# Mixing products put behind the preceding dense step, one product for the cached forget sums, and a vector's load moved to POOL

## The chip, the cores and the metric

One core of one Trainium2 chip runs one inference step. The metric is the device time of one execution in microseconds (us). Engines are named as in the profile: PE (TensorE, products), ACT (ScalarE), DVE (VectorE), POOL (GpSimd), SP (SyncE, which only issues DMAs here).

## What is computed

A hybrid encoder of two layers steps 256 new frames of one stream and 16 frames of each of 8 running streams, which makes 384 tokens, three tiles of 128.

```python
# layer 0: one projection, two kinds of attention, one output projection
fq, fk, fv, fz, logf, sq, sk, sv, sz = ab_project(rmsnorm(h, norm0_g), w_in0, b_forget)
F_all = cumsum(concat([cache_fox_logf, logf]), axis=1)       # forget sums, cached rows included
go = fox_core(fq, k_all, v_all, F_all[:, P:], F_all, qpos, kpos)
to = sb_core(sq, sk_all, sv_all, qpos, kpos)
h  = h + concat([go * silu(fz), to * silu(sz)]) @ w_out0
# layer 1: gated MLP with mixing over positions
p  = rmsnorm(h, norm1_g) @ w_in1                              # u, v, z of 4096 columns each
u, v, z = p[..., :C], layernorm(p[..., C:2*C], ln_g, ln_b), p[..., 2*C:]
mixed = einsum('gts,bnsgc->bntgc', tril(w_sp), v) + b_sp      # 16 groups of 256 columns
h  = h + (u * mixed * silu(z)) @ w_out1
y  = rmsnorm(h, final_g)
```

Everything is fp32.

## The kernel before

All large products run as three products of parts: a value is split into `hi`, rounded by ACT (L84 for weights, L90 for activations), and `lo`, what DVE has left (L86 and L91). For each weight tile of 128x512 and each token tile, PE does hi by hi (L100), hi by lo of the weight (L101) and lo of the activation by hi (L102). `dense_nat` runs over pairs `kp` of weight tiles; a pair is 18 products. Weights come by SP into `raw` (five buffers), and `whi` and `wlo` have four buffers each, so ACT can split a weight tile only when PE is done with the fourth before it.

A scheduler sets the order on each engine from the program and its own estimate; `tc.issue_after(x)` orders an instruction behind `x` if both are on the same engine. Engines run strictly in that order.

The change touches the end of layer 1. The 4096 columns are worked in eight blocks of 512, by `prepare(c)`, a generator whose steps are hooked between the pairs of dense products by `first_plan` and `later_plan`:

- `load_v`, `normalise`: POOL loads v, DVE normalises it (L1159, L1160), POOL loads what it needs;
- `turned_weights`, `split_values`: w_sp is turned and split (`wTh`, `wTl`), v is split (`vh` by ACT, `vl` by DVE);
- mixing: twelve products on PE, L1258 (vh, wTh), L1259 (vl, wTh) and L1260 (vh, wTl), six with 512 columns and six with 256, in four banks `a`; DVE multiplies each bank into `gate` (L1262);
- POOL writes `gate` to memory as `md` (three DMAs, L1268) and reads it back as `blk` (four, L1271), in order to turn it;
- DVE turns blk into `gTt` (L1275), and ACT and DVE split that into two slots, the chunk's hi and lo (L90, L91), which are the weights side of the dense products with w_out1.

So block c of the mixing becomes chunk c of w_out1's products: `out1(0, 8)` takes chunks 0 and 1, `out1(8, 8)` 2 and 3, `out1(16, 8)` 4 and 5, `out1(24, 4)` 6. Ahead of `out1(16, 8)` POOL also loads the final norm's vector (two DMAs of final_g) and three tiles of the last weights (w_out1). `last_product` holds the last product of the last pair that the program has written.

The forget sums of the cached rows are in `forget()`: `clf` holds the cached logs as [128 positions, 8 streams, 8 heads]; eight fp32 products (L440), one for each head, multiply it with a triangle `UT`, and two evictions (L444) and two DMAs (L445) store the result. At the start, `graw` (norm0_g, 16x128) comes by ACT's queue (L232), is transposed by PE (L258) between the transpositions of x (L263) and copied to `gT`, which DVE uses when it evicts x; `keep_warm` (L226) adds products of ones that nothing reads.

Of the kernel before, what the change touches and what calls it, by code (L numbers as in the profile page):

```python
# [15 lines left out]
P = 128  # L16
# [21 lines left out]
def tile_hybrid_step(  # L38
# [96 lines left out]
                G.dma_start(dst[32 * j:32 * j + 32, :, 32 * a:32 * a + 32], trn[32 * a:32 * a + 32, :, 32 * j:32 * j + 32])  # L135


    ident = cpool.tile([P, P], F32, name="ident")
    make_identity(nc, ident)
    ones = cpool.tile([P, P], F32, name="ones")  # L140
# [28 lines left out]
    with ExitStack() as l0:  # L169
        lc = l0.enter_context(tc.tile_pool(name="l0c", bufs=1, reuse_waits="tile"))  # L170
        lp = l0.enter_context(tc.tile_pool(name="l0p", bufs=2, reuse_waits="tile"))

        graw = lc.tile([KT, 2, P], F32, name="graw")
        def gains(j):
            gb = bank()
            PE.transpose(gb[:, :KT], graw[:, j, :], ident[:KT, :KT])
# [51 lines left out]
        keep_warm(6)  # L228
        for half in range(2):
            load_piece(0, half, nc.scalar)  # L230
            if not half:
                nc.scalar.dma_start(graw[:, 0, :], norm0_g.rearrange("(k p) -> k p", p=P))  # L232
            load_raw()
        load_piece(1, None, nc.scalar)
        load_raw()
# [15 lines left out]
        def x_transposes(k):  # L251
            if k < FB:
                b = bank()
                for tb in range(NT):
                    if k == 0 and tb == 2:

                        gb = bank()
                        then("PE", lambda: PE.transpose(gb[:, :KT], graw[:, 0, :], ident[:KT, :KT]))  # L258
                        then("DVE", lambda: V.tensor_copy(gT[:, :KT], gb[:, :KT]))
                        keep_warm(1)  # L260
                        b2 = bank()
                    bt = b if k or tb < 2 else b2
                    then("PE", lambda: PE.transpose(bt[:, tb * P:(tb + 1) * P], xs[k // 4][:, tb, k % 4 * P:k % 4 * P + P], ident))  # L263
            else:
                b = xblk[k]
            gcol = gT[:, k:k + 1]
            hi, lo = hhi[k // 4][:, k % 4, :], hlo[k // 4][:, k % 4, :]
            if k:
                high = then("ACT", lambda: S.activation(hi, b[:, :T], AF.Copy, scale=gcol))
            else:  # L270

                parts = (b, slice(0, 2 * P)), (b2, slice(2 * P, T))
                for bt, ts in parts:
                    high = then("DVE", lambda: V.tensor_scalar(out=hi[:, ts], in0=bt[:, ts], scalar1=gcol, scalar2=None, op0=ALU.mult))
                for bt, ts in parts:
                    low = then("DVE", lambda: V.scalar_tensor_tensor(out=lo[:, ts], in0=bt[:, ts], scalar=gcol, in1=f32(hi[:, ts]), op0=ALU.mult, op1=ALU.subtract))
                return high, low
            return high, then("DVE", lambda: V.scalar_tensor_tensor(out=lo, in0=b[:, :T], scalar=gcol, in1=f32(hi), op0=ALU.mult, op1=ALU.subtract))
# [132 lines left out]
        def forget(o):  # L411
            z = lc.tile([P, NT, 8], F32, name="fz")
            for tb in range(NT):
                V.scalar_tensor_tensor(out=z[:, tb, :], in0=o[tb][:, 256:264], scalar=rstd[:, tb:tb + 1], in1=bfg, op0=ALU.mult, op1=ALU.add)
            e = lc.tile([P, NT, 8], F32, name="fe")
            S.activation(e, z, AF.Abs)
            S.activation(e, e, AF.Exp, scale=-1.0)
            S.activation(e, e, AF.Ln, bias=1.0)
            V.scalar_tensor_tensor(out=logf, in0=z, scalar=0.0, in1=e, op0=ALU.min, op1=ALU.subtract)
            G.dma_start(flf_p.rearrange("o (t p) h -> p (o t) h", p=P), logf[:, :2, :])  # L420
            G.dma_start(flf_s.rearrange("b q h -> (b q) h"), logf[:, 2, :])

            yield
            b3 = bank()
            PE.matmul(b3[:8, :2 * P], lhsT=logf[:, 0, :], rhs=UT, start=True, stop=False)
            PE.matmul(b3[:8, P:2 * P], lhsT=logf[:, 1, :], rhs=UT[:, :P], start=False, stop=True)
            bs = bank()
            PE.matmul(bs[:8, :P], lhsT=logf[:, 2, :], rhs=BT, start=True, stop=True)
            for b_ in range(8):
                PE.matmul(bs[:8, P + b_:P + b_ + 1], lhsT=clf[:, b_, :], rhs=ones[:, 0:1], start=True, stop=True)  # L430
            tot = lc.tile([8, 8], F32, name="ftot")
            V.tensor_copy(tot, bs[:8, P:P + 8])
            FT = lp.tile([8, 2 * T], F32, tag="pr", name="FT")[:, :T]
            V.tensor_copy(FT[:, :2 * P], b3[:8, :2 * P])
            V.tensor_tensor(out=FT[:, 2 * P:].rearrange("h (b q) -> h b q", q=16), in0=bs[:8, :P].rearrange("h (b q) -> h b q", q=16),
                            in1=tot.unsqueeze(2).broadcast_to([8, 8, 16]), op=ALU.add)
            for hg in range(2):
                b5 = bank()
                for hh in range(4):
                    PE.matmul(b5[:8, hh * P:(hh + 1) * P], lhsT=clf[:, :, 4 * hg + hh], rhs=UT[:, :P], start=True, stop=True)  # L440
                hs = slice(4 * hg, 4 * hg + 4)
                b5v = b5[:8].rearrange("b (h p) -> b h p", p=P)
                nFc = lp.tile([8, 4, P], F32, tag="KT", bufs=4, name=nm("nFc"))
                S.activation(nFc, b5v, AF.Copy, scale=-1.0)  # L444
                G.dma_start(nFcd[:, hs, :], nFc)  # L445
            yield
            b4 = bank()
            for tb in range(NT):
                PE.transpose(b4[:, tb * 8:(tb + 1) * 8], FT[:, tb * P:(tb + 1) * P], ident[:8, :8])
            V.tensor_copy(Fnat, b4[:, :24].rearrange("p (t h) -> p t h", h=8))  # L450
            gains(1)
            nFT = lp.tile([8, 5 * P], F32, tag="PT", name="nFT")[:, :T]
            V.tensor_scalar(out=nFT, in0=FT, scalar1=-1.0, scalar2=None, op0=ALU.mult)
            G.dma_start(nFd, nFT)
# [412 lines left out]
    with ExitStack() as l1:  # L867
# [365 lines left out]
        def prepare(c):  # L1233

            with ExitStack() as behind:
                for i in read:
                    behind.enter_context(tc.issue_after(i))
                load_v(c)
                norm = normalise(c)
                next(norm)  # L1240
                gate = kept.get(c)
                if gate is None:
                    gate = lp.tile([P, NT, 512], F32, tag="gate", name=nm("gate"))
                    G.dma_start(gate, gd[c])
                wr = spatial_weights(c)
            yield
            for _ in norm:
                yield
            wh, wl = turned_weights(wr)
            yield  # L1250
            vh, vl = split_values(c)
            yield
            for i in range(2):
                cs = slice(i * 256, i * 256 + 256)
                for j, tbs in ((0, slice(0, 2)), (1, slice(2, 3))):
                    n = tbs.stop - tbs.start
                    m = bank()[:, :n * 256].rearrange("p (t c) -> p t c", t=n)
                    PE.matmul(m, lhsT=wh[:, j, i, :], rhs=vh[:, tbs, cs], start=True, stop=False)  # L1258
                    PE.matmul(m, lhsT=wh[:, j, i, :], rhs=vl[:, tbs, cs], start=False, stop=False)  # L1259
                    PE.matmul(m, lhsT=wl[:, j, i, :], rhs=vh[:, tbs, cs], start=False, stop=True)  # L1260
                    gh = gate[:, tbs, cs]
                    V.scalar_tensor_tensor(out=gh, in0=m, scalar=bcol[:, j, 2 * c + i:2 * c + i + 1], in1=gh, op0=ALU.add, op1=ALU.mult)  # L1262
            yield
            with ExitStack() as behind:
                for i in read:
                    behind.enter_context(tc.issue_after(i))
                for tb in range(NT):
                    G.dma_start(md[c][:, tb * P:(tb + 1) * P, :].rearrange("k t d -> t k d"), gate[:, tb, :].rearrange("p (k d) -> p k d", k=4))  # L1268
            blk = lp.tile([P, 4, T], F32, tag="trn", name=nm("blk"))
            for j in range(4):  # L1270
                read[:] = [G.dma_start(blk[32 * j:32 * j + 32].rearrange("p k (a d) -> p (k a) d", d=32),  # L1271
                                       md[c][:, :, 32 * j:32 * j + 32].rearrange("k (a p) d -> p (k a) d", p=32)).ins]
            yield
            gT = lp.tile([P, 4, T], F32, tag="gTt", bufs=1, name=nm("gTt"))
            V.transpose(out=gT.rearrange("p k t -> p (k t)"), in_=blk.rearrange("p k t -> p (k t)"))  # L1275
            hi, lo = slot().rearrange("p (k t) -> p k t", k=4), slot().rearrange("p (k t) -> p k t", k=4)
            split(hi, lo, gT)
            ghi.append(hi)
            glo.append(lo)
# [170 lines left out]
```

## Time and profile before

| what | value |
|---|---|
| median of three runs | 1741.54 us (1739.94 to 1743.31) |
| profiled execution | 1739.83 us |
| its span, first to last instruction | 1738.1 us |
| mean granted clock of PE | 0.999 |
| PE busy | 1726.9 us, 99% of the span |
| DVE, ACT, POOL busy | 1290.2, 834.7, 355.7 us |

The span is what a trace can explain; 1.7 us lie around it. The engines work side by side, so their busy times don't add up: only what is on the way of the engine that ends last counts.

### The profile page before, as it was taken

To read this page: it belongs to the slowest core of one execution; us is meant where nothing else is said; L and a number is where in the kernel's file an instruction comes from. 1 tells how busy PE (TensorE), PEld (TensorE's weight loads), DVE (VectorE), ACT (ScalarE), POOL (GpSimd) and SP (SyncE) were. 2 spreads that over 40 slices of the span, in tenths; PEclk is the share of its full clock that TensorE was granted. 3 is DMA by queue.
4 is the path that set the end of the run, shared out by engine and by line. 5 is a ranking of instruction groups with operands and counts; after the bars stand their busy time and mean duration, and the time that the engine had idled before them with its cause. 6 is when DMAs were issued, how large, how long until landed. Compare 5 with 4: busy or idle time off the path is not lost. (4 is left out here: it accounts for less than half of the span.)

```text
span 1738.1 us, 24002 instructions
## 1 busy us (share of the span) xinstructions
PE 1726.9 (99%) x8325; PEld 1428.0 (82%) x8325; DVE 1290.2 (74%) x1794; ACT 834.7 (48%) x1271; POOL 355.7 (20%) x501
## 2 busy tenths in 40 slices
PE   9999999999999999999999999999999999999998
PEld 8988888888888888888888888888888887888887
DVE  6337566448348545589999999999998887688766
ACT  5435344337336344455555555555554544444344
POOL 6435544212312211100000100000000033423200
PEclk9999999999999999999999999999999999999999
DMA  8788989869877867669988989888988678798553
GB/s 232 184 233 196 276 213 220 232 190 208 237 211 188 254 199 166 184 200 334 315 300 299 310 282 317 291 288 272 319 290 273 228 222 275 235 291 279 176 159 115
DMA packets 234523, 421.25 MB, mean 242 GB/s; under 512 B 22137, under 2 KB 65633, under 8 KB 234401
## 3 DMA queue, kind: packets, MB, share of 16 engines
q1 hardware_dynamic: 174992, 312.40, 57.4%
q0 software_dynamic: 28576, 91.18, 19.7%
q10 hardware_dynamic: 30832, 16.13, 3.2%
q8 instruction: 65, 1.06, 0.3%
q14 instruction: 58, 0.47, 0.1%
HBM read 372.78 MB, written 46.72 MB: 241 GB/s over the span
## 5 line engine op out<-in xcount | busy, mean ns | idle before, releaser
L101 PE MATMUL d<-wlo,slot 128*128 128x512 f32 x1389 | 540.7, 390 | 0.0
L102 PE MATMUL d<-whi,slot 128*128 128x512 f32 x1389 | 540.3, 390 | 0.4 <-DVE slot L91 0.4
L86 DVE TENSOR_TENSOR wlo<-raw,whi 128x512 fp32r<-128x512 f32 x450 | 308.9, 696 | 306.3 <-ACT whi L84 305.1
L84 ACT ACTIVATE whi<-raw 128x512 fp32r<-128x512 f32 x450 | 281.9, 630 | 456.2 <-PE d L102 365.0
L100 PE MATMUL d<-whi,slot 128*128 128x512 f32 x1389 | 492.7, 391 | 0.0
L90 ACT ACTIVATE shi<-sraw 128x1024 fp32r<-128x1024 f32 x280 | 296.0, 1062 | 262.2 <-DVE sraw L970 111.8
L91 DVE TENSOR_TENSOR slo<-sraw,shi 128x1024 fp32r<-128x1024 f32 x280 | 336.9, 1221 | 27.0 <-ACT shi L90 25.7
L100 PEld LDWEIGHTS d<-whi,slot 128*128 128x128 f32 x1389 | 260.5, 188 | 56.9 <-issue 1.4
L102 PEld LDWEIGHTS d<-whi,slot 128*128 128x128 f32 x1389 | 260.7, 188 | 54.9 <-DVE slot L91 0.6
L101 PEld LDWEIGHTS d<-wlo,slot 128*128 128x128 f32 x1389 | 260.8, 188 | 54.2 <-DVE wlo L86 0.6
L958 PE MATMUL a<-slo,slot 128*128 128x512 f32 x720 | 280.3, 389 | 0.0
L957 PE MATMUL a<-shi,slot 128*128 128x512 f32 x720 | 264.8, 391 | 0.6 <-ACT shi L90 0.4
L970 DVE TENSOR_TENSOR sraw<-sraw,sraw 128x1024 f32<-128x1024 f32 x160 | 195.2, 1220 | 1.0 <-DMA sraw<-in_w_in_dram 0.5
L957 PEld LDWEIGHTS a<-shi,slot 128*128 128x128 f32 x720 | 135.0, 188 | 33.6 <-ACT shi L90 4.8
L958 PEld LDWEIGHTS a<-slo,slot 128*128 128x128 f32 x720 | 135.2, 188 | 27.7
L959 PE MATMUL a<-shi,slot 128*128 128x512 f32 x400 | 155.7, 389 | 0.0
L959 PE MATMUL a<-shi,suml 128*128 128x512 f32 x320 | 124.5, 389 | 0.0
L959 PEld LDWEIGHTS a<-shi,slot 128*128 128x128 f32 x400 | 75.1, 188 | 15.8
L1056 POOL DMA_DIRECT2D gd<-slot x6 | 3.3, 554 | 346.3 <-DVE slot L898 346.3
L464 POOL DMA_DIRECT2D slot<-d x48 | 44.1, 925 | 131.0 <-DMA d<-slot 53.9
L959 PEld LDWEIGHTS a<-shi,suml 128*128 128x128 f32 x320 | 60.1, 188 | 12.5
L957 PE MATMUL d<-shi,slot 128*128 128x512 f32 x160 | 62.3, 389 | 0.0
(316 smaller groups left out, 1843.2 us busy)
## 6 DMA issues: line engine op xcount, KB each, us to landing
sraw<-in_w_in_dram SPq DMA_DIRECT2D x320, 512.0 KB, 5.1
raw<-in_w_in_dram SPq DMA_DIRECT2D x320, 256.0 KB, 3.9
raw<-in_w_out_dram SPq DMA_DIRECT2D x175, 256.0 KB, 3.9
slot<-d POOLq DMA_DIRECT2D x48, 192.0 KB, 5.7
d<-slot ACTq DMA_DIRECT2D x24, 256.0 KB, 3.9
vd<-slot POOLq DMA_DIRECT2D x8, 768.0 KB, 4.7
v<-vd POOLq DMA_DIRECT2D x8, 768.0 KB, 8.1
blk<-md POOLq DMA_DIRECT2D x32, 192.0 KB, 6.4
```

The lines of the kernel that those rows point to most:

```text
L84: highs.append(S.activation(hi, raw, AF.Copy).ins)
L86: splits.append(V.tensor_tensor(out=lo, in0=raw, in1=f32(hi), op=ALU.subtract).ins)
L90: S.activation(hi_out, src, AF.Copy)
L91: return V.tensor_tensor(out=lo_out, in0=src, in1=f32(hi_out), op=ALU.subtract).ins
L100: PE.matmul(o, lhsT=his[k][:, t], rhs=hi[:, 0, :], start=(k == first), stop=False)
L101: PE.matmul(o, lhsT=his[k][:, t], rhs=lo[:, 0, :], start=False, stop=False)
L102: mm = PE.matmul(o, lhsT=los[k][:, t], rhs=hi[:, 0, :], start=False, stop=(k == last))
L464: r = G.dma_start(blk[32 * j:32 * j + 32].rearrange("p h (a d) -> p (h a) d", d=32), d[:, :, 32 * j:32 * j + 32].rearrange("h (a p) d -> p ...
L957: PE.matmul(o, lhsT=xh, rhs=hi[:, j, :], start=(opens and u + j == 0), stop=False)
L958: PE.matmul(o, lhsT=xh, rhs=lo[:, j, :], start=False, stop=False)
L959: PE.matmul(o, lhsT=xl, rhs=hi[:, j, :], start=False, stop=(ends and u == 3 and j == 1))
L970: return V.tensor_tensor(out=out, in0=x, in1=y, op=op)
```

## The change

Three edits. The first of each bank's mixing products is ordered behind `last_product[0]`, on PE. The eight products of the cached forget sums become one with 64 columns, with one eviction and one DMA. `graw` is allocated first of all and its load is POOL's first DMA; PE transposes it ahead of the x transpositions; a `keep_warm(1)` is dropped.

```diff
+    graw = cpool.tile([KT, 2, P], F32, name="graw")
+    G.dma_start(graw[:, 0, :], norm0_g.rearrange("(k p) -> k p", p=P))
     ident = cpool.tile([P, P], F32, name="ident")
...
-        graw = lc.tile([KT, 2, P], F32, name="graw")
...
-            if not half:
-                nc.scalar.dma_start(graw[:, 0, :], norm0_g.rearrange("(k p) -> k p", p=P))
...
                 b = bank()
+                if k == 0:
+                    gb, b2 = bank(), bank()
+                    then("PE", lambda: PE.transpose(gb[:, :KT], graw[:, 0, :], ident[:KT, :KT]))
+                    then("DVE", lambda: V.tensor_copy(gT[:, :KT], gb[:, :KT]))
                 for tb in range(NT):
-                    if k == 0 and tb == 2:
-
-                        gb = bank()
-                        then("PE", lambda: PE.transpose(gb[:, :KT], graw[:, 0, :], ident[:KT, :KT]))
-                        then("DVE", lambda: V.tensor_copy(gT[:, :KT], gb[:, :KT]))
-                        keep_warm(1)
-                        b2 = bank()
...
-            for hg in range(2):
-                b5 = bank()
-                for hh in range(4):
-                    PE.matmul(b5[:8, hh * P:(hh + 1) * P], lhsT=clf[:, :, 4 * hg + hh], rhs=UT[:, :P], start=True, stop=True)
-                hs = slice(4 * hg, 4 * hg + 4)
-                b5v = b5[:8].rearrange("b (h p) -> b h p", p=P)
-                nFc = lp.tile([8, 4, P], F32, tag="KT", bufs=4, name=nm("nFc"))
-                S.activation(nFc, b5v, AF.Copy, scale=-1.0)
-                G.dma_start(nFcd[:, hs, :], nFc)
+            b5 = bank()
+            PE.matmul(b5[:64, :P], lhsT=clf.rearrange("p b h -> p (b h)"), rhs=UT[:, :P], start=True, stop=True)
+            nFc = lp.tile([64, P], F32, tag="KT", bufs=4, name=nm("nFc"))
+            S.activation(nFc, b5[:64, :P], AF.Copy, scale=-1.0)
+            G.dma_start(nFcd.rearrange("b h p -> (b h) p"), nFc)
...
-                    PE.matmul(m, lhsT=wh[:, j, i, :], rhs=vh[:, tbs, cs], start=True, stop=False)
+                    with tc.issue_after(last_product[0]):
+                        PE.matmul(m, lhsT=wh[:, j, i, :], rhs=vh[:, tbs, cs], start=True, stop=False)
                     PE.matmul(m, lhsT=wh[:, j, i, :], rhs=vl[:, tbs, cs], start=False, stop=False)
```

The scheduler then also orders other engines anew. Lines behind the first edit have other numbers in the changed kernel (mixing L1251 to L1253, md L1261, blk L1264, turn L1268). Three places follow; the number at the end of a name tells one tile from another of that name.

PE, in the first pair of w_out1's products that takes chunk 1 (its hi is slot_13251, its lo slot_13252), before:

```order
L102 MATMUL d_13218<-whi_13263,slot_13116 128x512
L1258 MATMUL a_13414<-vh_13339,wTh_13291 128x512
L1258 MATMUL a_13419<-vh_13339,wTh_13291 128x256
...
L1260 MATMUL a_13424<-vh_13339,wTl_13292 128x512
L100 MATMUL d_13216<-whi_13311,slot_13251 128x512
L101 MATMUL d_13216<-wlo_13313,slot_13251 128x512
...
L101 MATMUL d_13218<-wlo_13313,slot_13251 128x512
L1259 MATMUL a_13419<-vl_13340,wTh_13291 128x256
...
L1260 MATMUL a_13429<-vh_13339,wTl_13292 128x256
L102 MATMUL d_13216<-whi_13311,slot_13252 128x512
```

The same place after, with chunk 1's hi as slot_13238 and its lo as slot_13239:

```order
L101 MATMUL d_13205<-wlo_13252,slot_13102 128x512
L102 MATMUL d_13205<-whi_13250,slot_13103 128x512
L100 MATMUL d_13203<-whi_13298,slot_13238 128x512
L101 MATMUL d_13203<-wlo_13300,slot_13238 128x512
L100 MATMUL d_13204<-whi_13298,slot_13238 128x512
L101 MATMUL d_13204<-wlo_13300,slot_13238 128x512
L100 MATMUL d_13205<-whi_13298,slot_13238 128x512
L101 MATMUL d_13205<-wlo_13300,slot_13238 128x512
L102 MATMUL d_13203<-whi_13298,slot_13239 128x512
```

The twelve mixing products of block 2 have left; they stand three pairs of weight tiles (54 products) later, all together.

ACT, around the hi of chunk 5 (slot_14577 before, read by PE from the product 3916 of the dense ones on), before:

```order
L84 ACTIVATE whi_14553<-raw_14551 128x512
L84 ACTIVATE whi_14583<-raw_14581 128x512
L90 ACTIVATE slot_14577<-gTt_14575 128x1536
L84 ACTIVATE whi_14589<-raw_14587 128x512
L84 ACTIVATE whi_14635<-raw_14633 128x512
L84 ACTIVATE whi_14641<-raw_14639 128x512
L90 ACTIVATE vh_14663<-v_14290 128x512 x2
L84 ACTIVATE whi_14673<-raw_14671 128x512
L90 ACTIVATE vh_14663<-v_14290 128x512
```

And after, where the same hi is slot_14564:

```order
L84 ACTIVATE whi_14576<-raw_14574 128x512
L84 ACTIVATE whi_14622<-raw_14620 128x512
L90 ACTIVATE wTh_14604<-wT_14601 128x512
L84 ACTIVATE whi_14628<-raw_14626 128x512
L90 ACTIVATE vh_14650<-v_14277 128x512 x3
L84 ACTIVATE whi_14660<-raw_14658 128x512
L90 ACTIVATE slot_14564<-gTt_14562 128x1536
L84 ACTIVATE whi_14666<-raw_14664 128x512
```

The chunk's hi moved behind the weights of its own first pair (whi_14622, whi_14628), block 6's wTh and vh, and one more weight tile.

POOL, the DMAs of block 5 (md_7092 before), before:

```order
L1268 DMA md_7092<-gate_13952 128x4x128 x3
L1271 DMA blk_14394<-md_7092 32x48x32 x4
L1148 DMA v_14621<-vd_7078 128x1536
L1154 DMA lg_14623<-in_sgu_ln_g_dram 128x512
L1155 DMA lg_14623<-in_sgu_ln_b_dram 128x512
L1210 DMA wr_14626<-in_w_sp_dram 32x8x32 x2
L1326 DMA slot_14534<-in_final_g_dram 128x1024
L1326 DMA slot_14536<-in_final_g_dram 128x1024
L1332 DMA slot_14538<-in_w_out_dram 128x512 x3
```

And after (md_7079):

```order
L1261 DMA md_7079<-gate_13939 128x4x128 x3
L1319 DMA slot_14521<-in_final_g_dram 128x1024
L1319 DMA slot_14523<-in_final_g_dram 128x1024
L1325 DMA slot_14525<-in_w_out_dram 128x512 x3
L1264 DMA blk_14381<-md_7079 32x48x32 x4
L1140 DMA v_14608<-vd_7065 128x1536
```

The five loads for the end now stand between the write of block 5 and its reading back.

## The prediction

> **What bounds the kernel now.** I read the page's totals first, then what TensorE (PE) waited for, then busy time by stretches, and last the timeline where a stretch fell short.
>
> ```profile
> span 1738.1 us, 24002 instructions
> PE 1726.9 (99%) x8325; PEld 1428.0 (82%) x8325; DVE 1290.2 (74%) x1794; ACT 834.7 (48%) x1271; POOL 355.7 (20%) x501
> PE a L1259 <- DVE vl L91: 1.5, 1, 1.5
> PE d L102 <- DVE slot L91: 0.4, 1, 0.4
> 1450.00:1500.00 50.00, 48.10 (x213) 39.07 (x212) 35.19 (x56) 22.37 (x37) 19.27 (x29) 1.00 0.84 265
> 1580.00:1630.00 50.00, 50.00 (x224) 41.44 (x223) 39.85 (x62) 18.60 (x31) 17.45 (x25) 1.00 0.75 236
> ```
>
> PE is the bound: 99% busy, and a stretch such as 1580 to 1630 is 50.00 full (the columns of the last rows: stretch, length, busy time and count of PE, PEld, DVE, ACT, POOL, granted clock, DMA). So an instruction taken off PE is worth its time, one taken off another engine is worth nothing, and whatever makes PE wait costs in full. The hole that concerns the change lies in 1450 to 1500, at 48.10. Its two waits (rows three and four: us in all, times, longest) stand in the timeline of PE. Columns there: start, duration, instruction, and in brackets the idle time before it and who ended it.
>
> ```profile
> 1457.83 0.39 PE L102 MATMUL d<-whi,slot 128*128 128x512 f32 x1
> ...
> 1460.77 0.39 PE L102 MATMUL d<-whi,slot 128*128 128x512 f32 x1
> 1461.02 1.25 PE L1258 MATMUL a<-vh,wTh 128*128 128x512 f32 x4
> 1463.73 0.49 PE L1259 MATMUL a<-vl,wTh 128*128 128x512 f32 x1 [1.45 <-DVE vl L91]
> ...
> 1464.53 0.40 PE L1260 MATMUL a<-vh,wTl 128*128 128x512 f32 x1
> 1464.76 0.39 PE L100 MATMUL d<-whi,slot 128*128 128x512 f32 x1
> ...
> 1466.15 0.28 PE L1259 MATMUL a<-vl,wTh 128*128 128x256 f32 x1
> 1466.26 0.28 PE L1260 MATMUL a<-vh,wTl 128*128 128x256 f32 x1
> ...
> 1467.21 0.50 PE L102 MATMUL d<-whi,slot 128*128 128x512 f32 x1 [0.43 <-DVE slot L91]
> ```
>
> Durations overlap, so prices go by distance of starts. The first two rows are 13 products apart: 2.94 / 13 = 0.226 us for a dense 512 product. A mixing product takes 0.23 (1464.53 to 1464.76) with 512 columns and 0.11 (1466.15 to 1466.26) with 256. A block's twelve, six of each, are 6 x 0.23 + 6 x 0.11 = 2.1 us. From 1461.02 to 1467.21 (6.2 us) PE did these twelve and six dense products (1.4): 3.5 us of work, 2.7 lost.
>
> Why PE could do no better there is on the engines that split chunk 1 into hi and lo:
>
> ```profile
> 1461.40 1.26 ACT L84 ACTIVATE whi<-raw 128x512 fp32r<-128x512 f32 x2
> 1462.56 1.47 ACT L90 ACTIVATE slot<-gTt 128x1536 fp32r<-128x1536 f32 x1
> 1465.40 1.76 DVE L91 TENSOR_TENSOR slot<-gTt,slot 128x1536 fp32r<-128x1536 f32 x1
> ```
>
> ACT makes chunk 1's hi from 1462.56 to 1464.03, DVE its lo until 1467.16. The dense products from 1464.76 read the hi, the L102 at 1467.21 reads the lo. So the mixing of block 2 filled a wait that chunk 1 sets.
>
> **The change, part by part.**
>
> *Forget sums, -1.5 us.*
>
> ```profile
> L440 PE MATMUL a<-sums,clf x16: 270/272/273, 70.5 to 72.1; 128*8 128x128 f32 x16
> ```
>
> Eight fp32 products leave 16 records, two passes each, (72.1 - 70.5) / 15 = 0.107 us apart: 1.7 us. The new product streams the same 128 columns under 64 weight columns instead of 8: two passes, 0.2 us. PE is full here, so 1.5 us go. The one eviction and one DMA that remain instead of two each lie beside PE; I give them nothing. Bounds: 0 if PE waits for something there, -1.7.
>
> *Mixing at chunk 1, +2.1 us.* In the new order block 2's twelve products stand 54 dense products later, and directly behind the last product of chunk 0 come the six that need chunk 1's hi. On ACT and DVE the order around this place is as before, and hi still stands behind two whi conversions that wait for a PE product just ahead. So hi comes at about 1464.05 and lo at 1467.2, as before. PE waits from 1461.25 to 1464.05, does six products (to 1465.4), and waits again until 1467.2. The stage ends when it ended, but 2.1 us of mixing are still to do, and they are done later at full pace with nothing to hide under. The wait on vl that the change removes gave nothing back, since chunk 1 is late next. Bounds: +2.1, or 0 if ACT gets to hi earlier by as much. I take the upper end, for the rows above leave ACT no idle time between 1461.40 and 1464.03.
>
> [...] The wait would be some 2.8 us of idle PE. The trace shows the clock after that stall and around PE's last work:
>
> ```profile
> 1464.40:1467.80 3.40, 2.97 (x16) 2.32 (x15) 2.75 (x3) 0.00 (x0) 0.00 (x0) 1.00 0.96 330
> 1730.50:1734.00 3.50, 0.01 (x1) 0.00 (x0) 2.20 (x9) 1.63 (x4) 0.66 (x1) 1.00 0.02 6
> 1734.00:1738.00 4.00, 0.00 (x0) 0.00 (x0) 0.00 (x0) 0.00 (x0) 0.00 (x0) 0.54 0.69 257
> ```
>
> 3.5 idle microseconds at full clock, and then half; the stall of 1.45 left it at 1.00. 2.8 lies between, nearer to the one that took the clock. In the sum I leave the clock alone, since the fall that is shown needed more idle time than I forecast; a fall is a rival below. [...]
>
> *Chunk 5, +2.7 us.* The later mixing also changed the order on other engines. Before, PE and its suppliers stood so:
>
> ```profile
> 1603.15 0.84 PE L100 MATMUL d<-whi,slot 128*128 128x512 f32 x3
> 1595.46 1.49 ACT L90 ACTIVATE slot<-gTt 128x1536 fp32r<-128x1536 f32 x1 [0.59 <-DVE gTt L1275]
> 1599.99 1.31 ACT L84 ACTIVATE whi<-raw 128x512 fp32r<-128x512 f32 x2 [2.53 <-PE d L102]
> 1601.21 1.14 ACT L90 ACTIVATE vh<-v 128x512 fp32r<-128x512 f32 x2
> 1602.25 0.62 ACT L84 ACTIVATE whi<-raw 128x512 fp32r<-128x512 f32 x1
> 1597.72 1.75 DVE L91 TENSOR_TENSOR slot<-gTt,slot 128x1536 fp32r<-128x1536 f32 x1
> ```
>
> PE's first use of chunk 5's hi is at 1603.15, 6.2 us after ACT made it. In the new order that ACT instruction stands behind seven others: whi, wTh, whi, three vh, whi. With four whi buffers, the first of these whi waits for a product 14 places ahead of that first use: 1603.15 - 14 x 0.226 = 1599.99 for its start, some 1600.35 for its end (the 1599.99 row shows ACT waiting for PE in the same way). Seven instructions at 0.53 (1601.21 to 1602.25 is two) bring ACT to 1604.1, hi takes 1.49: 1605.6, 2.45 late. Lo follows on DVE with 1.75 until 1607.35; PE's six products between last until 1607.0, so 0.3 more. In all +2.7.
>
> That holds if the data is there. Rows of POOL, and issue to landing:
>
> ```profile
> 1573.40 2.25 POOL L1268 DMA_DIRECT2D md<-gate  x3 [5.99 <-DVE gate L1262]
> 1581.34 3.68 POOL L1271 DMA_DIRECT2D blk<-md  x4 [5.69 <-DMA md<-gate]
> slot<-in_final_g_dram POOLq DMA_DIRECT2D x2, 512.0 KB, 9.6
> blk<-md POOLq DMA_DIRECT2D x4, 192.0 KB, 6.0
> ```
>
> Block 5 mixes about 3.4 us later (15 dense products), so md is written from 1576.8; then POOL now issues the two final_g loads and three of w_out1, ahead of the four blk reads. By 9.6 for the first load (issued at 1579.1, landed 1588.7), and the last blk read behind it with 6.0 and an issue of 0.9, chunk 5 is there at about 1595.6. DVE's transposition (1.8) then ends well ahead of ACT's 1604.1; the margin is 6 us. Bounds of this part: 0, if ACT runs ahead of my count by 2.5; +5.5 with the data late (below).
>
> *The other blocks, 0.*
>
> ```profile
> 1507.11 1.49 ACT L90 ACTIVATE slot<-gTt 128x1536 fp32r<-128x1536 f32 x1
> 1525.22 0.39 PE L100 MATMUL d<-whi,slot 128*128 128x512 f32 x1
> ```
>
> Block 2 moves furthest: its last product goes from dense product 3345 to 3393, 11 us by 0.226. Without the hole it skips and with PE's waits the gate comes some 8 us later. Its chunk's hi is there at 1508.6, and PE wants it at 1525.22, 16.6 later. Block 1's chunk is the one PE waits for at 1461, and its block moves by 4.1. Its way goes over POOL:
>
> ```profile
> 1449.47 3.67 POOL L1271 DMA_DIRECT2D blk<-md  x4 [6.19 <-PE d L102]
> ```
>
> The read back had waited 6.19 for a PE product that frees its buffer, so 4.1 are swallowed there. Blocks 4 and 6 move by less (18 and 12 products: 4.1 and 2.7), blocks 0, 3 and 7 finish where they did. All hidden; if one were not, the price is what is left over of its move, up to 4.
>
> *First norm's vector, 0.*
>
> ```profile
> 0.41 0.10 POOL L1437 MEMSET const-uint8-127<- 128x1 uint8 x1
> 1.30 0.47 ACTq L232 DMA_DIRECT2D graw<-in_norm_g_dram  x1
> 4.42 0.29 PE L258 MATMUL a<-ident,graw 16*128 16x16 f32 x1
> 5.72 1.59 PE L302 MATMUL d<-whi,slot 128*128 128x512 f32 x3
> 4.89 0.63 ACT L282 ACTIVATE whi<-raw 128x512 fp32r<-128x512 f32 x1 [2.81 <-DMA raw<-in_w_in_dram]
> ```
>
> The first product (5.72) follows ACT's whi (until 5.52), which waited for raw; graw isn't on that path. POOL can issue its first DMA behind the memory sets that end at 0.5, ACT issued at 1.30, so graw should land no later than before (used at 4.42). If it lands late, the x transpositions now stand behind it in PE's order; I bound that at +0.5, the distance from 4.42 to the end of whi left over. If it is early, raw still bounds: -0.3 at best. The keep-warm product that goes ran in PE's wait for raw.
>
> **Sum.** -1.5 + 2.1 + 2.7 + 0 = +3.3 us on the profiled execution's 1739.83 (span 1738.1): 1743.1. The median of the runs, 1741.54, lies 1.7 above that execution; against it I expect 1744.8. About 0.2% (3.5 us) is what a measurement of this kernel can tell from no change, so the forecast lies at the edge of slower.
>
> **Rivals.**
>
> - *The stall goes.* If chunk 1's hi and lo come as PE reaches them, the 2.7 lost at 1461 vanish, chunk 5 stays hidden, and with the forget sums it is -4.2: 1737.3. For it: the longest wait on the list is the mixing's own. Against it: ACT's rows have no gap. It decides if hi is ready by 1461.3 instead of 1464.0.
> - *Chunk 5 stays hidden.* -1.5 + 2.1 = +0.6: 1742.1. For it: 6.2 us of slack before. It takes ACT 2.5 us ahead of my count.
> - *Chunk 5's data is late.* If the loads ahead of it are slower and blk lands at 1605, the transposition ends at 1606.8, hi at 1608.3: 5.2 late, with lo 5.5, and the sum +6.1: 1747.6. It decides from a landing past 1602.3 on.
> [...]
> - *Neither wait shows:* the forget sums alone, 1740.0.
>
> **Chances.** Forecast 0.42, which I halve between same (0.22) and slower (0.20), as +3.3 is at the edge. Chunk 5 hidden 0.18 (same). Data late 0.16, clock 0.07 (slower). Stall gone 0.12, of which 0.07 faster by over 0.2%. Neither 0.05 (same). Together faster 0.07, same 0.50, slower 0.43. The range 1739.5 to 1749.5 leaves out most of the stall-gone case and a late landing beyond 1607. The forecast case's own range is 1743 to 1747.
>
> **What would show it.** In the profile after: a wait of about 2.8 us of the first L100 on chunk 1's slot from ACT L90 near 1462, followed by one of about 1.7 on DVE L91; the L1259 wait gone; another pair of about 2.4 and 0.3 near 1605 (times shifted by the first terms); one product of 64 columns in place of L440's eight; the first dense product within 0.3 of 5.72. It is wrong if chunk 5's hi is made before PE has reached chunk 4's last products, or if PE finds other work in the new holes.

## The result and the profile after

The change made the kernel slower: 1759.07 us (1756.27 to 1760.21, four runs) against 1741.42 before, ratio 1.0098 with a 95% interval of 1.0086 to 1.011. That is 15 to 19 us, where 3.3 were forecast. The range ended at 1749.5.

The totals and PE's waits of the kernel after (us in all, times, longest):

```profile
span 1756.8 us, 23966 instructions
PE 1734.6 (99%) x8309; PEld 1430.1 (81%) x8309; DVE 1288.7 (73%) x1794; ACT 833.9 (47%) x1270; POOL 357.1 (20%) x501
PE d L100 <- ACT slot L90: 5.1, 2, 2.8
PE d L100 <- ACT whi L84: 4.6, 3, 1.9
PE a L255 <- POOL diag L340: 1.3, 1, 1.3
PE d L102 <- DVE slot L91: 0.7, 1, 0.7
```

The products are 16 fewer, yet PE's busy time is 7.7 longer: some products ran at half clock (0.50 for 13.7 us in all between 1467 and 1624). The two waits for a slot's hi (2.8 and 2.3) are the ones the prediction named. The 4.6 for whi (3.5 of it at chunk 5) it did not have.

Where the time went shows in the starts of the same dense product in two traces, counted over L100 to L102. The table gives how much later each trace reaches it than the trace before (us); a step from one column to the next is what the place between them costs. Product 1 ends the start, 136 stands behind the forget sums, 3214 to 3394 is the place at chunk 1 with block 2's mixing, 3790 to 3978 the place at chunk 5 with block 6's mixing.

| product | 1 | 136 | 2000 | 3214 | 3394 | 3790 | 3978 | 4311 |
|---|---|---|---|---|---|---|---|---|
| start in the profile before | 8.86 | 81.47 | 541.35 | 1432.44 | 1478.22 | 1574.59 | 1619.37 | 1696.99 |
| after | 1.77 | 0.36 | 0.38 | 3.16 | 5.91 | 6.42 | 18.64 | 18.60 |
| e1, forget sums only | 1.27 | -0.15 | -0.15 | 1.69 | 1.73 | 1.73 | 1.73 | 1.73 |
| e2, start only | 2.65 | 2.67 | 3.49 | 4.45 | 4.46 | 4.46 | 4.46 | 4.46 |
| e3, mixing only | -0.32 | 0.25 | 0.33 | 0.65 | 4.26 | 4.78 | 14.64 | 14.59 |
| e4, loads behind | 3.53 | 2.12 | 2.44 | 3.49 | 9.06 | 11.47 | 12.08 | 12.05 |
| e5, hi first | 3.04 | 1.70 | 2.41 | 3.76 | 9.18 | 11.39 | 21.53 | 21.50 |
| e6, hole filled | 3.27 | 2.07 | 2.69 | 4.03 | 6.19 | 7.35 | 18.24 | 18.37 |
| e7, vector by ACT | 1.70 | 1.67 | 1.68 | 3.73 | 3.88 | 3.86 | 3.86 | 3.91 |
| e8, ordering without blocks 2 and 5 | -0.16 | -0.15 | -0.15 | -0.14 | 1.05 | 1.08 | 1.00 | 0.97 |
| e9, loads ahead | -0.55 | 0.20 | 0.20 | 2.32 | 3.17 | 3.16 | 5.85 | 5.85 |
| e10, forget sums and chunk 1's hi | -0.37 | -1.15 | -0.84 | 0.35 | -0.57 | -0.61 | -0.61 | -0.61 |

After, 12.2 of the 18.6 arise at chunk 5, 2.75 at chunk 1, 1.8 at the start, and -1.4 at the forget sums. The 2.8 between products 2000 and 3214 can't be laid to the change: e1 and e10 lose 1.8 and 1.2 there without an edit near it, and e3 0.3. One profile is that uncertain in this stretch.

**Chunk 5.** Timelines of ACT, PE and POOL after; then what ACT waited for, and how long SP's weight loads took, between 1580 and 1612:

```profile
1596.89 0.63 ACT L84 ACTIVATE whi<-raw 128x512 fp32r<-128x512 f32 x1 [4.38 <-DMA raw<-in_w_out_dram]
1600.94 0.63 ACT L84 ACTIVATE whi<-raw 128x512 fp32r<-128x512 f32 x1 [3.42 <-DMA raw<-in_w_out_dram]
1604.32 0.63 ACT L84 ACTIVATE whi<-raw 128x512 fp32r<-128x512 f32 x1 [2.75 <-DMA raw<-in_w_out_dram]
1607.35 0.63 ACT L84 ACTIVATE whi<-raw 128x512 fp32r<-128x512 f32 x1 [2.40 <-DMA raw<-in_w_out_dram]
...
1605.01 0.50 PE L100 MATMUL d<-whi,slot 128*128 128x512 f32 x1 [1.92 <-ACT whi L84]
1608.03 1.22 PE L100 MATMUL d<-whi,slot 128*128 128x512 f32 x2 [1.56 <-ACT whi L84]
1609.48 0.63 PE L102 MATMUL d<-whi,slot 128*128 128x512 f32 x1
1609.90 0.63 PE L100 MATMUL d<-whi,slot 128*128 128x512 f32 x1
...
1620.09 0.50 PE L100 MATMUL d<-whi,slot 128*128 128x512 f32 x1 [2.27 <-ACT slot L90]
...
1584.76 2.25 POOL L1261 DMA_DIRECT2D md<-gate  x3 [9.46 <-DVE gate L1255]
1587.00 1.10 POOL L1319 DMA_DIRECT2D slot<-in_final_g_dram  x2
1588.09 1.61 POOL L1325 DMA_DIRECT2D slot<-in_w_out_dram  x3
1590.02 2.79 POOL L1264 DMA_DIRECT2D blk<-md  x3 [0.31 <-issue]
...
ACT whi L84 <- DMA raw<-in_w_out_dram: 14.8, 5, 4.4
DMA to landing us min/median/max: 2.5/10.6/15.8
```

POOL puts out its five loads without a pause, 1587.0 to 1589.7, and the reads back behind them. Before, the reads had started at 1581.34, and the five loads came behind them, from 1588.74 to 1594.7, each after a wait. In the traces of before and after no DMA of POOL starts earlier than 0.28 us behind the landing of the one eight places ahead of it (423 pairs in each); for the first two loads before, these were reads back, landed at 1588.2 and 1589.4 (the profile puts these two waits down to raw). Both queues are booked on the same 16 DMA engines: after, between 1586 and 1612, POOL's took 62.5% of them and SP's weight loads 31.6%. Rows of before, the last two between 1575 and 1605:

```profile
1588.74 0.57 POOL L1326 DMA_DIRECT2D slot<-in_final_g_dram  x1 [0.90 <-DMA raw<-in_w_out_dram]
1589.93 0.55 POOL L1326 DMA_DIRECT2D slot<-in_final_g_dram  x1 [0.62 <-DMA raw<-in_w_out_dram]
...
ACT whi L84 <- DMA raw<-in_w_out_dram: 3.5, 2, 2.2
DMA to landing us min/median/max: 2.5/7.2/9.4
```

The slowest load took 15.8 instead of 9.4, and ACT waited 14.8 for raw instead of 3.5. Five buffers of raw covered the 3.5; behind the 14.8, PE waited for whi. From 1608 on, products start 0.42 apart (1609.48 to 1609.90) instead of 0.226: the clock has fallen, to 0.50 from 1607.01 to 1613.84. An estimate from PE's starts parts the 12.2: some 5 us of waiting for whi and wlo, 2.4 for chunk 5's hi, and 4.6 of half clock (half of 1608.0 to 1613.8 and of 1620.7 to 1624.1).

**Chunk 1.** PE after, and busy time and clock in two stretches (the columns as in the prediction):

```profile
1464.29 0.39 PE L102 MATMUL d<-whi,slot 128*128 128x512 f32 x1
1467.46 0.80 PE L100 MATMUL d<-whi,slot 128*128 128x512 f32 x1 [2.79 <-ACT slot L90]
1468.06 0.63 PE L101 MATMUL d<-wlo,slot 128*128 128x512 f32 x1
1468.48 0.63 PE L100 MATMUL d<-whi,slot 128*128 128x512 f32 x1
...
1471.05 0.50 PE L102 MATMUL d<-whi,slot 128*128 128x512 f32 x1 [0.66 <-DVE slot L91]
1463.65:1467.06 3.41, 1.02 (x5) 0.52 (x3) 3.41 (x5) 3.41 (x6) 1.04 (x2) 1.00 1.03 408
1467.06:1470.47 3.41, 2.93 (x6) 1.82 (x6) 3.41 (x5) 0.35 (x1) 0.00 (x0) 0.50 1.01 331
```

The wait of 2.8 came as forecast. The second wait is 0.7 and not 1.7, because the six products between took 0.42 each at a clock of 0.50.

**Start.** PE and POOL after:

```profile
1.34 0.70 POOL L139 DMA_DIRECT2D graw<-in_norm_g_dram  x1 [0.83 <-POOLq L1430]
5.37 0.25 PE L255 MATMUL a<-ident,graw 16*128 16x16 f32 x1 [1.33 <-POOL diag L340]
6.91 1.62 PE L298 MATMUL d<-whi,slot 128*128 128x512 f32 x3
```

POOL's first DMA went out at 1.34, no sooner than ACT's (1.30), and the vector was used at 5.37 instead of 4.42. The profile puts the wait ahead of it down to POOL, but the vector's own landing fits: its load took 3.9 here and 3.1 before, and in e2 the same wait, 2.1, is put down to this DMA. The first product starts at 6.91 instead of 5.72.

### The profile page after: what moved, and what is told of

Same layout as the page of the kernel before. It is cut to its first block, busy times and chain, and to the rows that moved or that the text cites. A ratio compares the mean times of both kernels' runs of the same rounds, so it can differ in the third digit from the quotient of the medians.

```text
span 1756.8 us, 23966 instructions
## 1 busy us (share of the span) xinstructions
PE 1734.6 (99%) x8309; PEld 1430.1 (81%) x8309; DVE 1288.7 (73%) x1794; ACT 833.9 (47%) x1270; POOL 357.1 (20%) x501
## 5 line engine op out<-in xcount | busy, mean ns | idle before, releaser
L102 PE MATMUL d<-whi,slot 128*128 128x512 f32 x1389 | 541.1, 390 | 0.7 <-DVE slot L91 0.7
L100 PE MATMUL d<-whi,slot 128*128 128x512 f32 x1389 | 498.2, 394 | 9.7 <-ACT slot L90 5.1
L100 PEld LDWEIGHTS d<-whi,slot 128*128 128x128 f32 x1389 | 261.9, 189 | 69.9 <-ACT whi L84 6.8
L102 PEld LDWEIGHTS d<-whi,slot 128*128 128x128 f32 x1389 | 261.7, 188 | 56.1 <-DVE slot L91 1.4
L951 PEld LDWEIGHTS a<-shi,slot 128*128 128x128 f32 x400 | 75.1, 188 | 15.8
```

What stands on the lines that cost most here:

```text
L100: PE.matmul(o, lhsT=his[k][:, t], rhs=hi[:, 0, :], start=(k == first), stop=False)
L102: mm = PE.matmul(o, lhsT=los[k][:, t], rhs=hi[:, 0, :], start=False, stop=(k == last))
L951: PE.matmul(o, lhsT=xl, rhs=hi[:, j, :], start=False, stop=(ends and u == 3 and j == 1))
```

## Experiments

**The three edits apart.** e1 keeps the forget sums, e2 the start, e3 the mixing, each on the kernel before.

```diff
 e1: the hunk of forget() alone
 e2: the hunks of graw, its load, x_transposes and keep_warm alone
 e3: the hunk of the mixing alone
-                    PE.matmul(m, lhsT=wh[:, j, i, :], rhs=vh[:, tbs, cs], start=True, stop=False)
+                    with tc.issue_after(last_product[0]):
+                        PE.matmul(m, lhsT=wh[:, j, i, :], rhs=vh[:, tbs, cs], start=True, stop=False)
```

> The kernel before with only the cached forget sums as one product. In the trace after, that part shows as 1.4 us (the lead over before went from +1.77 to +0.36 across it). If its price is just that, the span is 1736.7 and the time 1.4 below before. If the edit also causes the two holes that the trace after shows near 560 us (1.85) and 880 us (1.0), it comes out 1.4 above before instead.

> The kernel before with only the vector's load on POOL and its transposition put first. Theory: POOL lands the vector 0.9 later than ACT's queue did (5.3 against 4.4), the x transpositions behind it wait, and the clock rises later, so the time is 1.2 to 2.5 above before. Rival, the prediction's: raw still bounds and the time is as before, within 0.5. If the hole near 560 us comes from here, 1.9 more.

> The kernel before with only the mixing products ordered behind the preceding dense products. The trace after shows +2.7 at chunk 1 and +12 from block 5's mixing to block 6's: if these are this edit's own, the time is 14 to 16 above before. If half of the loss after comes from the three edits together, 8 or less.

Measured: e1 1740.82, ratio 0.9998 (0.9988 to 1.0007), so -2.1 to +1.2; its trace gains 1.42 from product 1 to 136 and loses 1.8 between 2000 and 3214, where other traces lose too. e2 1744.04, 1.0018 (1.0008 to 1.0027): +3.1. e3 1755.52, 1.0087 (1.0072 to 1.0102): +15.1. The sum, -0.3 + 3.1 + 15.1 = 17.9, agrees with the 17.1 of the whole. The mixing's order is the cost, the start comes second, and the forget sums can't be told from nothing by time.

**e4: POOL's loads back behind the reads.** On the changed kernel:

```diff
+                    with tc.issue_after(read[-1]):
-                    G.dma_start(fg, final_g[j * 1024:(j + 1) * 1024].partition_broadcast(P))
+                        G.dma_start(fg, final_g[j * 1024:(j + 1) * 1024].partition_broadcast(P))
...
-                    G.dma_start(x[:, j, :], wlast(*ck))
+                    with tc.issue_after(read[-1]):
+                        G.dma_start(x[:, j, :], wlast(*ck))
```

> The changed kernel with the five loads on POOL (two of final_g, three of w_out1) ordered behind block 5's four reads back, as they stand in the kernel before; the scheduler then also puts chunk 5's hi on ACT back to 44 products of margin. Theory: the loss at chunk 5 comes from these loads standing ahead and crowding the weight loads, so 11 to 12 of the 17.6 go: about 1747. Rival: block 5's later mixing makes the loss whatever POOL's order is: 1757 to 1759. With the prediction's mechanism alone (hi late on ACT, no crowding) 2.7 would go: 1756.

Measured: 1748.39, 1.0047 (1.003 to 1.0063), so 8.9 (by the ratios) to 10.7 (by the medians) less than the changed kernel. POOL, then ACT's wait for raw and the weight loads between 1585 and 1617, then PE's wait:

```profile
1594.73 3.68 POOL L1264 DMA_DIRECT2D blk<-md  x4 [2.68 <-DMA md<-gate]
1598.40 1.12 POOL L1320 DMA_DIRECT2D slot<-in_final_g_dram  x2
ACT whi L84 <- DMA raw<-in_w_out_dram: 1.5, 1, 1.5
DMA to landing us min/median/max: 2.5/6.6/8.9
PE d L100 <- DVE slot L1194: 0.4, 1, 0.4
```

The last row is all that PE waits for between 1590 and 1625. From product 3790 to 3978 the delay grows by 0.6 instead of 12.2, though block 5 still mixes late. The edit also let the scheduler put chunk 5's hi back to its early place on ACT, so this run alone does not part the two; e5 does. Nor is it the burst as such: POOL's nine DMAs leave back to back here too (1594.73 to 1601.2), only with the reads first, and no weight load took more than 8.9. The loads' place ahead of the reads is what costs; why it weighs so much is not shown.

**e5: chunk 5's hi first on ACT, POOL's order kept.** On the changed kernel, the whi conversions of the pair stand behind the hi (the hook returns what they stand behind):

```diff
+            if k0 == 16:
+                h[2] = lambda f=h[2]: f() or [his[5]]
```

> The changed kernel, with ACT's conversion to chunk 5's hi put ahead of the three weight conversions and block 6's vh that stood before it; POOL's order with the five loads ahead is kept. It parts the two costs at chunk 5. Theory: the crowded weight loads (waits of PE for whi, some 6 us with the fall of the clock) stay, and the wait for hi (2.3, and 1.6 of half clock behind it) goes: 1755 to 1757. If the late hi were the whole loss, as the prediction's step had it, 11 go: 1748. If it is a part of the crowding that only shows there, nothing goes: 1759.

Measured: 1758.13, 1.0089 (1.0072 to 1.0106); against the changed kernel no difference that shows. PE's waits between 1600 and 1630, of e5, then chunk 5's hi on ACT and PE's first product with it:

```profile
PE d L100 <- ACT whi L84: 5.2, 3, 1.9
PE d L101 <- DVE wlo L86: 1.1, 2, 0.9
1621.35 1.49 ACT L1270 ACTIVATE slot<-gTt 128x1536 fp32r<-128x1536 f32 x1 [1.05 <-DVE gTt L1268]
...
1623.41 0.96 PE L100 MATMUL d<-whi,slot 128*128 128x512 f32 x3 [1.45 <-ACT whi L84]
```

The wait for hi is gone by name, but hi is not early: it now waits for DVE's turning of blk, which stands in DVE's order behind splits that waited 2.4 to 2.6 each for whi, and the 1.45 at 1623.41 is PE's wait for the weights that now follow hi. The place costs 10.1, 2.1 less than after. So hi's place on ACT is worth about 2 of the 12.2 at most, and the time doesn't show it; the 10 that stay go with the loads' place (e4).

**e6: the hole at chunk 1 filled.** On the changed kernel:

```diff
+                    for i in range(10):
...
+                            PE.matmul(b[:, :P], lhsT=ones, rhs=ones, start=True, stop=True)
```

> The changed kernel with ten fp32 products of ones, 2.1 us on PE, put behind the last product ahead of chunk 1, where PE waits 2.8. Their result is not read. Theory: the clock falls there because its window of 3.4 us is only 30% busy; filled to over 80% it stays at 1.0, and the place costs 2.1 instead of 2.8 to 5. Rival: the clock follows something else, and the products behind the hole run 0.43 apart again.

Measured: one run, 1758.3. PE and the clock at the place, of e6:

```profile
1465.11 2.40 PE L1335 MATMUL a<-ones 128*128 128x128 f32 x20
1468.30 0.50 PE L100 MATMUL d<-whi,slot 128*128 128x512 f32 x1 [0.80 <-ACT slot L90]
1466.69:1470.10 3.41, 2.47 (x14) 1.67 (x12) 3.41 (x6) 1.56 (x2) 0.03 (x1) 1.00 1.02 366
```

PE is busy for 2.47 of the 3.41 us of the last row (72%, where over 80% was expected), the clock stayed at 1.00, and the place cost 2.2 (4.03 to 6.19). This is read from the trace alone; the time is of one run, and chunk 5 costs 10.9 in it. In the four traces with the hole left open the place cost 2.75 (after, with the clock at 0.50 from 1467.06 to 1470.47), 3.6 (e3), 5.6 (e4) and 5.4 (e5). So the 2.1 of the prediction fits the price of the mixing that lost its cover. That the rest goes with the clock is shown by rows for after; for e3 to e5 it is an estimate from these costs.

**e7: the vector by ACT's queue again**, with PE's new order at the start, on the kernel before (the lines show its difference from e2):

```diff
-    G.dma_start(graw[:, 0, :], norm0_g.rearrange("(k p) -> k p", p=P))
...
+            if not half:
+                nc.scalar.dma_start(graw[:, 0, :], norm0_g.rearrange("(k p) -> k p", p=P))
```

> The kernel before with the vector's transposition put ahead of the x transpositions and the one keep-warm product dropped, but the vector still loaded by ACT's queue. Theory: the loss at the start comes from POOL's late landing; here the first product is back at 5.7 to 6.3 and the time within 1 of before. Rival: it comes from the order on PE, and the time is 3 above before.

Measured: 1742.92, 1.0008 (0.9999 to 1.0017): +1.4, between the two theories. The first product starts at 6.65; in the five traces with the whole new start at 6.91 to 7.78 (e2 7.66); in the six with the old start at 5.72 to 6.32 (before 5.72, e1 6.32). By those starts both parts cost, the order on PE some 0.3 to 0.9 and POOL's landing some 0.3 to 1.1 more; by time they can't be parted surely.

**e8: the ordering for all blocks but 2 and 5**, on the kernel before:

```diff
+                        if c not in (2, 5):
+                            behind_dense.enter_context(tc.issue_after(last_product[0]))
```

> The kernel before with the mixing ordered behind the dense products for all blocks but 2 and 5. Theory: the ordering costs at these two places alone; POOL's loads stay behind the reads back, and the time is as before, within 1. Rival: a share of the 15 us of the ordering lies in the other blocks, and 3 or more remain.

Measured: 1741.75, 1.0000 (0.9991 to 1.001). Six of eight blocks can be ordered at no price that shows, and at no gain.

**e9: the loads ahead, nothing else**, on the kernel before: the five loads, in a function `end_loads`, are put out between block 5's write and its reads back.

```diff
+            ahead = end_loads(written) if c == 5 else None
             blk = lp.tile([P, 4, T], F32, tag="trn", name=nm("blk"))
...
+                if ahead is not None:
+                    behind_loads.enter_context(tc.issue_after(ahead))
```

> The kernel before with one thing moved on POOL: the two loads of final_g and the three of w_out1 stand between block 5's write to memory and its four reads back, as in the changed kernel; mixing, forget sums and start are as before, and chunk 5's hi keeps 37 products of margin on ACT. Theory: this order alone crowds the weight loads, and the time is 5 to 10 above before, with waits of PE for whi behind the DMA of raw near 1590 to 1600. Rival: it needs the later mixing too (less time for the same bytes), and the time is within 1.5 of before.

Measured: 1745.56, 1.0024 (1.0014 to 1.0034): +4.2, under the 5 to 10 expected and clear of the rival. In its trace 2.7 of it stand at the place (3.16 to 5.85).

```profile
1578.91 1.10 POOL L1237 DMA_DIRECT2D slot<-in_final_g_dram  x2
1585.36 3.69 POOL L1287 DMA_DIRECT2D blk<-md  x4 [3.74 <-DMA md<-gate]
ACT whi L84 <- DMA raw<-in_w_out_dram: 9.1, 4, 3.2
DMA to landing us min/median/max: 2.5/7.6/12.4
```

Here the reads back follow the loads after 3.7 us of waiting for md; in the changed kernel they follow after 0.3. ACT's wait for raw is 9.1, between the 3.5 of before and the 14.8 after. With e4 this makes four cases of what chunk 5 costs: early mixing with loads behind 0, late mixing with loads behind 0.6, early with loads ahead 2.7, late with loads ahead 12.2 (some 2 of it for hi's place on ACT, which moved too). The full loss needs both. Why the two multiply is open: that the reads follow the loads at once is a reading of the POOL rows, not tried by itself.

**e10: a version meant to beat both**, the kernel before with the forget sums as one product, and the whi conversions that stood ahead of chunk 1's hi put behind it:

```diff
+            if k0 == 0:
+                h[3] = lambda f=h[3]: f() or [his[1]]
```

> A version meant to beat both: the kernel before with the forget sums as one product, and ACT's conversions for the fourth pair of w_out1 ordered behind chunk 1's hi instead of ahead of it. By the traces the first is worth 1.4; the second brings hi 0.6 and lo about 1.2 earlier at the hole of 1461, so 2 to 2.6 in all (0.12 to 0.15%): 1739. Rival: the conversions that now wait are late at their own products, and nothing is left but the 1.4.

Measured: 1739.84, 0.9992 (0.9983 to 1.0001), where 2 to 2.6 were expected. The place at chunk 1 gained 0.9 in the trace (0.35 to -0.57), with this wait for hi left:

```profile
1463.82 0.50 PE L100 MATMUL d<-whi,slot 128*128 128x512 f32 x1 [1.20 <-ACT slot L1273]
```

It is 1.4 below before by the ratio, but the interval touches 1, so it isn't shown to be faster.

## Why the prediction was wrong

- *Forget sums, -1.5:* right by the traces, which give -1.4 (product 1 to 136, after and e1 alike); the time alone can't show it.
- *Chunk 1, +2.1:* the mechanism held, the size only with the clock held (2.2 in e6; six times 0.23 and six times 0.11 are 2.04). The step that failed is the weighing of the clock: "the fall that is shown needed more idle time than I forecast". I read 3.5 idle us as the shown need and gave a fall a chance of 0.07. After, it fell to 0.50 for 3.41 us behind the wait of 2.8, and the place cost 0.6 (after) to 3.4 (e4) more with the hole open than in e6.
- *Chunk 5, +2.7:* the failed step is "That holds if the data is there". I followed blk only, found 6 us of margin, and never asked what the five loads, put ahead of the reads, would do to SP's weight loads, which are booked on the same DMA engines (31.6% of them to POOL's 62.5%) and have PE behind them. The wait for hi that I priced at 2.45 came as 2.27, so that part of the term held; the late weights, which the sum has at nothing, and the half clock behind them made up the rest of the 12.2. That is more than twice the rival's 5.5, and that rival was for another transfer: blk's reads were slow too (12.9 instead of 6.0), but DVE's turning, at 1613.77, follows other work without a wait for them.
- *Start, 0:* wrong, +3.1 in e2. "POOL can issue its first DMA behind the memory sets that end at 0.5" failed: it went at 1.34. "I bound that at +0.5" failed because the x transpositions, queued behind the vector on PE, wait for it whole (the first starts at 5.55, at 3.84 before). The clock also rose later: to 1.00 at 7.1 in the profile before, at 9.6 in that after and, estimated from the starts of PE's products, at some 10.6 in e2. That PE's longer wait is the reason is argued; e1, with the old start, rose at some 9.1 by the same estimate.
- *Other blocks, 0:* right (e8).
- *The rivals:* "the stall goes" is out; the mixing's wait went and PE waited longer. The fall of the clock, 0.07 in the chances, happened: to 0.50 at chunk 1 (1467.06) and twice at chunk 5 (1607.01 and 1620.66).

## What to carry to other kernels

When an order changes, list each queue's new run of DMAs, and ask of each burst what else is on the same engines: here, loads that nobody waited for, put ahead of others, held up those that PE waited for (the slowest weight load took 15.8 instead of 9.4). A wait that an engine fills with other work isn't lost time: here the 2.1 us of mixing that had filled the wait at chunk 1 came back as 2.2 with the clock at 1.00 (e6). Nor does a hole's length alone give its price: with the clock at 0.50 behind it the same place cost 2.75 (after). Look at the granted clock behind each hole, too.

## What the runs showed that was not expected

The clock fell here without an idle stretch. In the traces of before and after its changes lie whole multiples of 3.41 us apart (after: 1467.06, 1470.48, 1607.01, 1613.84, 1620.66, 1624.08), so the rows take PE's busy time by stretches of that length. Rows of before, e8 and after:

```profile
1461.22:1464.63 3.41, 1.94 (x8) 1.19 (x8) 3.41 (x6) 2.80 (x4) 0.58 (x1) 1.00 1.01 372
1460.61:1464.02 3.41, 1.94 (x9) 0.98 (x8) 3.41 (x6) 3.06 (x6) 0.58 (x1) 1.00 1.02 412
1464.02:1467.43 3.41, 3.41 (x9) 2.63 (x10) 3.31 (x4) 0.52 (x1) 0.00 (x0) 0.50 1.02 332
1607.01:1610.42 3.41, 2.39 (x6) 1.91 (x7) 1.89 (x3) 1.21 (x2) 0.00 (x0) 0.50 1.04 340
1610.42:1613.84 3.42, 3.42 (x10) 2.65 (x9) 3.33 (x8) 0.05 (x1) 0.02 (x1) 0.50 0.58 202
```

Behind stretches with 1.02, 1.14 and 1.24 us busy of 3.41 (30%, 33% and 36%, all after) it fell to 0.50; behind 2.2 (65%, e7's chunk 1) it stayed at 1.00. Behind 1.94 (57%) it stayed before and fell in e8 and e9 (0.50 from 1464.02 and from 1466.54 on): the kernel before was as busy there as two that lost the clock, and what decides is not shown. Where it fell the place cost 1.2 (e8) and 0.9 (e9) more than before. At 0.50, a stretch with 2.39 busy (70%) was followed by another at 0.50, one with 2.93 (86%, chunk 1 after) and the full ones of 1610.42 and 1620.66 by 1.00. Where between these shares the clock turns is not shown.
